# Local attention scores over zero-padded keys, and linear attention's float32 products in two column halves

## The chip, the cores and the metric

The kernel runs on one core of one Trainium2 chip. The metric is device microseconds (us) of the whole program, the median of several executions. Engines are named as in the profile: PE is TensorE's matmuls, PEld its weight loads (the stationary operand), DVE VectorE, ACT ScalarE, POOL GpSimd, SP SyncE. "Records" are the instructions that the profiler saw: a float32 matmul of the program leaves two matmul records and two weight loads, a float32r matmul leaves one of each.

## The reference, cut to what matters

512 tokens of width 1024 go through a token-mixing block, a product-key expert layer, a gated delta rule layer and a short convolution layer. The change is in the first of these. There, the normed input is projected to many parts, and two kinds of attention are formed from them:

```python
# gated linear attention, 4 heads, dk 128, dv 256, chunks of 64 tokens
def step(state, xs):
    qi, ki, vi, di = xs
    out = jnp.einsum('bhtd,bhde->bhte', qi, state)
    state = di[..., None] * state + jnp.einsum('bhsd,bhse->bhde', ki, vi)
    return state, out
o = o_intra + o_inter            # o_intra = (masked q k) v inside a chunk
...
# sliding window attention, 16 heads of 64 sharing 4 key heads, blocks of 128 tokens
s = jnp.einsum('bnqhgd,bnkhd->bnhgqk', qb, kk) * (hd ** -0.5)   # kk: this block's keys and the last one's
...
p = jnp.exp(s - m)
```

Their outputs are gated, projected, merged and added to the stream.

## The kernel before

The function `mix` holds both attentions. Most large products are made from two float32r parts of each operand (a first part and the remainder), three matmuls a product, in `mm3` (L207, L208, L209); the weights come from DRAM into `wraw` and are split into `whi` on ACT (L89) and `wlo` on DVE (L92).

**Linear attention.** For each of the 4 heads, `gla_inside` forms what needs no state: cumulative gates (L353), masked scores (L378), keys transposed (L383). Then `gla_chunks` walks through 4 token tiles of two chunks each. Per tile it makes, all in plain float32: the product inside the chunks (L394, stationary 128 x 128, 256 columns moving, 16 in all), for each chunk the product of queries with the state (L398, stationary 128 x 64: its 64 result rows lie on half of the array's columns, 28 in all), and for each chunk the state's update (L402, its 64 tokens lie on half of the array's rows, 64 x 128 stationary, 28 in all). DVE adds the decayed state (L408), ACT evacuates (L412, L413). The order in this stage isn't written out by hand: a scheduler interleaves the projections that come later in the program (`tokspill`, through `mm3`) with the heads.

**Sliding window attention.** The keys' two float32r parts are kept feature-major in a tile `kp_`: `kh_`, the first part, is there twice, on both halves of the partitions; `kl_`, the second part, is there once, on partitions 0 to 63 for key heads 0 and 1 and on 64 to 127 for key heads 2 and 3. A query's two parts lie on the two halves of `qT`. So a score is made by one matmul over 128 partitions (L552: both parts of the query with the keys' first part) and a second over 64 (L553: the query's first part with the keys' second part):

```python
PE.matmul(b, qT[:, i], kh_[:, hg, ks], start=True, stop=False)
PE.matmul(b, qT[half_(w), i], kl_[half_(w), hg % 2, ks], start=False, stop=True)
```

`weights` does this for four heads, eight matmuls one after the other; it is called 16 times, of which 4 (block 0) have 128 key columns and 12 have 256. The keys are written by `read_keys` (transposes L504, ACT L507 for `kh_`, DVE L510 for `kl_`). In this stage the order on PE is written out by hand (`manual_schedule`, L639): 18 slots, in each `spread` (transposes of the weights of two slots earlier, L584), `queries_out` (L538, then ACT L541), `attend` (L599, L601), `weights`, and between these a fixed number of `mm3` steps of the gates' projections (`fill`). After the scores of a slot come DVE copies (L561, L562), the maximum, the exponentials on ACT (L574), and the scaling on POOL (L578), which the transposes of the second slot after wait for. The last projections in the stage (`out_steps`) use ACT's Silu (L622).

POOL fills the masked scores' tiles (L374), block 0's score tiles (L559) and takes the queries' second part (L532).

Of the kernel before, what the change touches and what calls it, by code (L numbers as in the profile page):

```python
# [16 lines left out]
P = 128  # L17
T = 512
# [11 lines left out]
def kernel(ctx: ExitStack, tc: tile.TileContext, A: dict, out: bass.AP):  # L30
# [24 lines left out]
    # ---------------------------------------------------------------- helpers  # L55
# [21 lines left out]
    share = {"every": 0, "n": 0}    # of the weights' second parts, every n-th by the pool engine  # L77

    def wchunk(ap, name="w"):
        """A [128, 2048] chunk of a weight matrix (8 row tiles, 256 columns) in two halves, each split  # L80
        into two float32r parts. For a token-major product the halves are along the rows, for a
        feature-major one along the columns."""
        for i in range(NK // HK):
            raw = wraw.tile([P, HK * 256], F32, name=name + "raw", tag="wraw")
            hi = wsp.tile([P, HK * 256], F32R, name=name + "hi", tag="whi")
            lo = wsp.tile([P, HK * 256], F32R, name=name + "lo", tag="wlo")
            with tc.high_priority(offset=WPRIO):
                nc.sync.dma_start(raw, ap[:, i * HK * 256:(i + 1) * HK * 256])
                S.activation(hi, raw, AF.Copy)  # L89
                share["n"] += 1  # L90
                pool_ = share["every"] and share["n"] % share["every"] == 0
                (GP if pool_ else V).tensor_tensor(lo, raw, f32(hi), op=ALU.subtract)  # L92
            yield i, hi, lo
# [4 lines left out]
    def rsqrt(ss, n, shape, name="rs", dst=None):  # L98
        """1/sqrt(ss*n + eps): a first guess from the exponent's bits, then Newton steps."""
# [16 lines left out]
    def rsqrt2(ss, n, name, dst=None):  # L116
        """the same for two columns on the pool engine, by its power"""
# [11 lines left out]
    def evac_split(hi, lo, p, scale):  # L129
        """hi + lo = p * scale, in two float32r parts."""  # L130
# [5 lines left out]
    class Stream:  # L136
        """The residual stream between two stages, [128, 4, 1024] token-major: in SBUF, in DRAM, 1/rms
        of every token, and the normed stream transposed, in two parts [128, 8, 512]. n: the stage
        that reads it."""
# [12 lines left out]
        def squares(self, tiles):  # L152
            """the sums of squares of every token of two token tiles"""
# [6 lines left out]
        def ready(self, t, ss):  # L160
            """token tiles t and t + 1 are complete; ss: their sums of squares"""
# [6 lines left out]
        def norm(self, t):  # L168
            """token tile t, normed and transposed"""
# [20 lines left out]
        def first_feat(self, ap, order=(0, 1)):  # L190
            """The token tiles of the second half, and proj_feat of the first chunk by halves."""
            w = [(m, *kview(x, NK)) for m, *x in wchunk(ap)]
            pp = [pj() for m in range(2)]
            for j in order:
# [4 lines left out]
                # The first start clears the whole bank.  # L199
# [28 lines left out]
    def proj_tok_last(aps, xs):  # L228
        """proj_tok whose token tiles end one after the other; yields them by pairs."""
# [22 lines left out]
    def proj_feat_steps(ap, xh, xl, by, n=T):  # L252
        """feature-major: [128 features, n tokens] for the two column tiles of a chunk."""
# [9 lines left out]
    def proj_tok_steps(aps, xs, by):  # L263
        """token-major: four [128 tokens, 256 columns]; aps: the chunks along K, xs: their operands."""
# [4 lines left out]
        # Two groups share a bank: the first matmul's start clears the whole bank, and the second  # L269
        # group's first write finds it cleared.  # L270
# [12 lines left out]
    # ---------------------------------------------------------------- token mixing  # L283
    def mix(X, O):
        w1 = A["w_in"]
        with ExitStack() as st:
# [56 lines left out]
            # ---- gated linear attention, head by head  # L343
# [5 lines left out]
            def gla_inside(h):  # L349
                """the parts of a head that need no state"""  # L350
# [35 lines left out]

            def gla_chunks(h, qx, ket, at, dec):
# [4 lines left out]
                for t in range(NT):  # L392
                    po = ps()[:, :256]
                    PE.matmul(po, at[:, t, :], gv[:, t, h * 256:(h + 1) * 256], start=True, stop=True)  # L394
                    for a in range(2):
                        n = 2 * t + a
                        if st_ is not None:
                            PE.matmul(po[64 * a:64 * a + 64, :], qx[:, n, :], st_, start=False,  # L398
                                      stop=True, skip_group_check=True)
                        if n < 7:  # L400
                            sp = ps()[:, :256]
                            PE.matmul(sp, ket[64 * a:64 * a + 64, t * P:(t + 1) * P], vh(t, a),  # L402
                                      start=True, stop=True)
# [41 lines left out]
            # ---- sliding window attention  # L445
# [31 lines left out]
            # Keys and queries in two float32r parts, feature-major: the keys' first part twice, on either  # L477
            # half of the partitions, and a query's two parts on the two halves; so one pass gives two of
            # the three products, and a second one the third. The second key head pair has the halves
            # swapped, for its keys' second part lies on the other half.  # L480
            kp_ = s16([P, 6, T], F32R, name="kp")
            kh_, kl_ = kp_[:, 0:4], kp_[:, 4:6]
# [12 lines left out]
            def read_keys(t):  # L495
# [12 lines left out]
                for w in range(2):  # L508
                    o, h = half_(w), slice(2 * w, 2 * w + 2)
                    V.tensor_tensor(kl_[o, :, s], p[o, h], f32(kh_[o, h, s]), op=ALU.subtract)  # L510
# [33 lines left out]
            def weights(n, hg, qT):  # L544
                """the softmax of four heads that share keys; the columns hold the tokens of block n up to the
                row and those of block n - 1 after it"""
                w = hg // 2
                sp = [ps(), ps()]
                ks = slice(max(0, n - 1) * P, (n + 1) * P)
                for i in range(4):  # L550
                    b = sp[i // 2][:, (i % 2) * 256 + (0 if n else P):(i % 2) * 256 + 256]
                    PE.matmul(b, qT[:, i], kh_[:, hg, ks], start=True, stop=False)  # L552
                    PE.matmul(b, qT[half_(w), i], kl_[half_(w), hg % 2, ks], start=False, stop=True)  # L553
# [50 lines left out]
            # ---- branch gates, output gate of the linear attention  # L604
# [31 lines left out]
            # Four heads a slot: their scores in one slot, the weighted sums two slots later; the tensor  # L636
            # engine's work in a fixed order, with the gates' projections in between.
# [31 lines left out]
            # ---- branches, merge  # L669
# [39 lines left out]
    # ---------------------------------------------------------------- product-key experts  # L709
    def peer(X, O):  # L710
        KD = 3                      # token tiles that go through all experts on the tensor engine
        ND = KD * P
        HS = 16                     # tokens of a staged block of gate matrices
        TB = 4                      # tokens of a block of one-hot rows
        with ExitStack() as st:
# [19 lines left out]
            # ---- the last token tile: its experts' rows by indirect DMA  # L735
# [37 lines left out]
            # ---- the other tiles through all experts: groups of five chunks, ten rows of experts  # L773
# [57 lines left out]
            # ---- scores and the 16 best keys of every head and half  # L831
# [36 lines left out]
            def route(t):  # L868
                """the 16 best experts of every head, their gates; yields every few operations"""
# [3 lines left out]
                # pairs (a, b) with (a+1)(b+1) <= 16: every other pair has 16 better or earlier ones  # L873
# [35 lines left out]
                # gates  # L909
# [21 lines left out]
                # indices and the gate's two parts, one row per (head, k), as float16  # L931
# [7 lines left out]
            def gate_matrices(t):  # L939
                """G[j, i] of every token of the tile, expert i * 128 + j"""  # L940
# [26 lines left out]
            # the tensor engine's projections at an even rate in between  # L967
# [41 lines left out]
    # ---------------------------------------------------------------- gated delta rule  # L1009
    def out_proj(aps, parts, X, O, wr, Y=None):  # L1010
        """X + rmsnorm(the projection (+ Y)) * w; aps[c]: the weights of 256 columns."""
# [38 lines left out]
    def conv_silu(p, wc, taps, tmp):  # L1050
        """Causal depthwise convolution along the free axis, one weight per partition and tap."""
# [7 lines left out]
    def gdn(X, O):  # L1059
# [6 lines left out]
        with ExitStack() as st:  # L1066
# [23 lines left out]
            # ---- keys and queries, feature-major and not normed: [dk, head, chunk, (k | q), 64]  # L1090
# [6 lines left out]
            def kq_mm(i):  # L1097
                """one tile of 128 columns of the projection; i: pair of key heads, (k, q), key head"""
# [26 lines left out]
            # ---- beta and g, token-major [128, 4, 16]  # L1125
# [53 lines left out]
            def g_rows():  # L1179
                # E[j, (h, t), i] = exp(G_i - G_j) for j <= i, else 0  # L1180
# [37 lines left out]
            def u_store(c, q):  # L1218
                """the diagonal blocks of U of key heads 2c and 2c + 1"""
# [8 lines left out]
            def rows(c):  # L1228
                """the factors of every token of key heads 2c and 2c + 1"""
# [56 lines left out]
            # ---- values (filler of the triangular solve)  # L1286
# [94 lines left out]
            # ---- R = (I + U)^-1: 32 x 32 diagonal blocks by substitution, (half, head, tile) on  # L1381
            # partitions
# [18 lines left out]
            # to rows on partitions by the tensor engine; the first block's transpose too  # L1401
# [12 lines left out]
            # the off-diagonal blocks: -R1 U12 R2; the two halves' blocks on a diagonal  # L1414
# [42 lines left out]
            # ---- the recurrence, two heads of a key head at a time  # L1457
# [27 lines left out]
            def recur(kh, vb, kd, oo):  # L1485
                """The chunks of a pair of heads; yields after each step that waits for another engine."""
# [90 lines left out]
            # Two pairs at a time, half a pair apart; the tensor engine's work in a fixed order, with  # L1577
            # the steps of the output gate's and the output's projections in between.
# [18 lines left out]
            def fill(x):  # L1597
                """the projections' steps up to the time x of the plan"""
# [44 lines left out]
    # ---------------------------------------------------------------- short convolution  # L1643
# [168 lines left out]
```

## Time and profile before

| | |
|---|---|
| median of 3 runs | 3065.36 us (3063.47, 3065.36, 3077.59) |
| profiled execution, first to last instruction | 3072.8 us |
| mean granted TensorE clock | 0.983 of full speed |
| PE busy / PEld / DVE / ACT / POOL | 96% / 81% / 64% / 40% / 22% |
| PE matmul records | 16274 |
| linear attention's chunks | about 141 to 203 us of the span |
| sliding window stage | about 255 to 460 us |

The profile holds one execution; no other time of it is recorded than its span. The share of busy time is over the whole span, and a busy PE is not PE at its peak: matmuls overlap, and the end of one is modelled. What a matmul costs in a row of matmuls is the distance from its start to the start of the next, which the timeline shows.

### The profile page before, as it was taken

Reading aid. Unit: us, or ns where it says so; the run is one execution under the profiler, and the core shown is the slowest. Engines: PE = TensorE matmul, PEld = TensorE weight load, DVE = VectorE, ACT = ScalarE, POOL = GpSimd, SP = SyncE. Lnnn points to the kernel's source line nnn. Section 1 sums busy time; section 2 is a strip of 40 time slices with the busy share of each in tenths; the row PEclk is TensorE's granted clock in tenths of the full one; section 3 lists DMA queues with packets and bytes.
Section 4 is the critical chain, followed back from the end, with each engine's and each line's share of the span. In section 5 each row is a group of like instructions: output and inputs, shape, how many; then the busy total and the mean of one; then the engine's idle time right before and its main releaser. Section 6 shows DMA issues by size and latency. Waiting matters only on the chain.

```text
span 3072.8 us, 42867 instructions
## 1 busy us (share of the span) xinstructions
PE 2943.9 (96%) x16274; PEld 2499.6 (81%) x16274; DVE 1972.4 (64%) x3798; ACT 1216.1 (40%) x2089; POOL 662.6 (22%) x583
## 2 busy tenths in 40 slices
PE   8999999998889999999899999999999999999998
PEld 6978778888889998777798888787866678888888
DVE  3348664499898776777787777658845554444432
ACT  3534473323345553333333333465343344332322
POOL 1001110002342312223454443134411202000000
PEclk9999999999999999999999999999999899999999
DMA  3213224333466779899999888446322313223222
GB/s 130 76 58 131 85 86 157 106 100 100 143 217 226 244 267 307 315 333 317 323 315 313 308 320 309 160 115 144 128 86 90 107 59 119 98 96 124 96 90 83
DMA packets 206919, 528.61 MB, mean 172 GB/s; under 512 B 38777, under 2 KB 84441, under 8 KB 202362
## 3 DMA queue, kind: packets, MB, share of 16 engines
q1 hardware_dynamic: 144018, 326.17, 32.5%
q0 software_dynamic: 43168, 155.27, 14.2%
q10 hardware_dynamic: 19528, 44.44, 3.9%
q8 instruction: 128, 2.10, 0.3%
q14 instruction: 77, 0.63, 0.1%
HBM read 464.49 MB, written 61.33 MB: 171 GB/s over the span
## 4 chain that ended last, share of the span: by engine, by line
PE 50%; DMA 9%; DVE 6%; issue 4%; ACT 2%; POOL 1%; SPq 0%; POOLq 0%; DVEq 0%; ACTq 0%
PE pp L207 12%; PE pp L208 11%; PE pp L209 11%; DMA wraw<-in_peer_v_dram 4%; DMA gath<-in_peer_v_rows_dram,ge 2%; PE ps L209 2%; PE ps L208 2%; PE ps L207 2%; DVE wlo L92 1%; PE ps L1495 1%; PE ps L1529 1%; DMA gath<-in_peer_u_rows_dram,ge 1%; DMA wraw<-in_peer_u_dram 1%; PE ps L954 1%; POOL gath L751 1%
## 5 line engine op out<-in xcount | busy, mean ns | idle before, releaser
L89 ACT ACTIVATE whi<-wraw 128x1024 fp32r<-128x1024 f32 x492 | 519.9, 1057 | 980.1 <-PE pp L208 555.1
L92 DVE TENSOR_TENSOR wlo<-wraw,whi 128x1024 fp32r<-128x1024 f32 x466 | 580.3, 1245 | 422.6 <-ACT whi L89 409.7
L209 PE MATMUL pp<-x2h,wlo 128*128 128x384 f32 (+2 forms) x1168 | 405.4, 347 | 23.7 <-DVE wlo L92 22.0
L207 PE MATMUL pp<-x2h,whi 128*128 128x384 f32 (+2 forms) x1168 | 407.6, 349 | 17.3 <-ACT whi L89 9.7
L208 PE MATMUL pp<-x2l,whi 128*128 128x384 f32 (+2 forms) x1168 | 404.2, 346 | 1.1 <-DVE x2l L188 1.1
L209 PE MATMUL ps<-whi,wtl 128*128 128x512 f32 x640 | 254.8, 398 | 8.5 <-DVE wtl L817 8.5
L208 PE MATMUL ps<-wlo,wth 128*128 128x512 f32 x640 | 254.9, 398 | 3.2 <-DVE wlo L92 3.2
L207 PE MATMUL ps<-whi,wth 128*128 128x512 f32 x640 | 253.8, 397 | 2.3 <-ACT whi L89 2.0
L209 PEld LDWEIGHTS pp<-x2h,wlo 128*128 128x128 f32 x1168 | 224.8, 193 | 34.7 <-DVE wlo L92 28.1
L751 POOL DMA_INDIRECT gath<-in_peer_u_rows_dram,ge x128 | 173.3, 1354 | 336.2 <-DVE gath L754 168.6
L207 PEld LDWEIGHTS pp<-x2h,whi 128*128 128x128 f32 x1168 | 225.3, 193 | 24.2 <-ACT whi L89 10.8
L751 POOL DMA_INDIRECT gath<-in_peer_v_rows_dram,ge x128 | 170.1, 1329 | 316.9 <-DVE gath L754 153.7
L208 PEld LDWEIGHTS pp<-x2l,whi 128*128 128x128 f32 x1168 | 225.2, 193 | 6.5 <-DVE x2l L188 1.6
L207 PE MATMUL pp<-x4h,whi 128*128 128x512 f32 (+1 forms) x528 | 202.4, 384 | 3.8 <-ACT x4h L187 3.8
L208 PE MATMUL pp<-x4l,whi 128*128 128x512 f32 (+1 forms) x528 | 202.7, 384 | 0.9 <-DVE x4l L188 0.9
L209 PE MATMUL pp<-x4h,wlo 128*128 128x512 f32 (+1 forms) x528 | 202.5, 384 | 0.0
L759 DVE SCALAR_TENSOR_TENSOR acc<-gath,w,acc 128x1024 f32<-128x1024 f32 x127 | 163.7, 1289 | 22.7 <-DMA gath<-in_peer_v_rows_dram,ge 22.5
L754 DVE SCALAR_TENSOR_TENSOR gath<-gath,grow 128x1024 f32<-128x1024 f32 x128 | 157.4, 1237 | 30.0 <-DMA gath<-in_peer_u_rows_dram,ge 29.8
L207 PE MATMUL pp<-x3h,whi 128*128 128x512 f32 (+1 forms) x400 | 168.4, 421 | 7.4 <-ACT x3h L187 5.7
L816 ACT ACTIVATE wth<-wt 128x384 fp32r<-128x384 f32 x128 | 66.8, 522 | 252.1 <-PE pp L208 154.5
L208 PE MATMUL pp<-x3l,whi 128*128 128x512 f32 (+1 forms) x400 | 156.4, 391 | 1.8 <-DVE x3l L188 1.8
L209 PE MATMUL pp<-x3h,wlo 128*128 128x512 f32 (+1 forms) x400 | 156.3, 391 | 0.0
(492 smaller groups left out, 6500.2 us busy)
## 6 DMA issues: line engine op xcount, KB each, us to landing
wraw<-in_peer_u_dram SPq DMA_DIRECT2D x128, 512.0 KB, 5.3
wraw<-in_peer_v_dram SPq DMA_DIRECT2D x128, 512.0 KB, 7.1
wraw<-in_sc_w_in_dram SPq DMA_DIRECT2D x64, 512.0 KB, 3.5
wraw<-in_w_in_dram SPq DMA_DIRECT2D x52, 512.0 KB, 4.0
Gd<-sgs ACTq DMA_DIRECT2D x24, 1024.0 KB, 6.5
wraw<-in_gdn_w_in_dram SPq DMA_DIRECT2D x48, 512.0 KB, 3.7
Gt<-Gd SPq DMA_DIRECT2D x12, 1920.0 KB, 15.8
Hd<-ht ACTq DMA_DIRECT2D x25, 384.0 KB, 4.5
```

What stands on the lines that cost most here:

```text
L89: S.activation(hi, raw, AF.Copy)
L92: (GP if pool_ else V).tensor_tensor(lo, raw, f32(hi), op=ALU.subtract)
L207: PE.matmul(p, lh, rh, start=first, stop=False, skip_group_check=skip)
L208: PE.matmul(p, lh, rl, start=False, stop=False, skip_group_check=skip)
L209: PE.matmul(p, ll, rh, start=False, stop=last, skip_group_check=skip)
L751: GP.indirect_dma_start(out=r, out_offset=None, in_=src, in_offset=bass.IndirectOffsetOnAxis(ap=idx3[:, k:k + 1], axis=0))
L754: V.scalar_tensor_tensor(r, r, 1.0, xn3, op0=ALU.mult, op1=ALU.mult, accum_out=h3[:, k:k + 1])
L759: V.scalar_tensor_tensor(acc3, r, w3[:, k:k + 1], acc3, op0=ALU.mult, op1=ALU.add)
L816: S.activation(wh, w, AF.Copy)
L954: PE.matmul(o, AB[:, 1, :, q], A2[:, 0, :, q], start=True, stop=False)
L1495: PE.matmul(B2[o, 0, v], Q[s_][o, u, :], vn[o, v], start=True, stop=True)
L1529: PE.matmul(B2[:, 1, v], kd[o, v, t, :], vn[o, v], start=True, stop=True)
```

## The change

Three things change, all in `mix`. The second part of the keys gets a slot for each of the four key heads, is filled with zeros by POOL, and is then written on the same half of the partitions as before; so the second product of a score runs over all 128 partitions, with the zero half adding nothing. The three float32 products of `gla_chunks` are each issued as two matmuls of 128 columns. Comments and docstrings are removed, which is not shown.

```diff
+            cols = [slice(0, P), slice(P, 2 * P)]
...
                     po = ps()[:, :256]
-                    PE.matmul(po, at[:, t, :], gv[:, t, h * 256:(h + 1) * 256], start=True, stop=True)
+                    for j, c in enumerate(cols):
+                        PE.matmul(po[:, c], at[:, t, :], gv[:, t, h * 256:(h + 1) * 256][:, c], start=j == 0,
+                                  stop=True, skip_group_check=True)
                     for a in range(2):
                         n = 2 * t + a
                         if st_ is not None:
-                            PE.matmul(po[64 * a:64 * a + 64, :], qx[:, n, :], st_, start=False,
-                                      stop=True, skip_group_check=True)
+                            for c in cols:
+                                PE.matmul(po[64 * a:64 * a + 64, c], qx[:, n, :], st_[:, c], start=False,
+                                          stop=True, skip_group_check=True)
                         if n < 7:
                             sp = ps()[:, :256]
-                            PE.matmul(sp, ket[64 * a:64 * a + 64, t * P:(t + 1) * P], vh(t, a),
-                                      start=True, stop=True)
+                            for c in cols:
+                                PE.matmul(sp[:, c], ket[64 * a:64 * a + 64, t * P:(t + 1) * P], vh(t, a)[:, c],
+                                          start=True, stop=True)
...
-            kp_ = s16([P, 6, T], F32R, name="kp")
-            kh_, kl_ = kp_[:, 0:4], kp_[:, 4:6]
+            kp_ = s16([P, 8, T], F32R, name="kp")
+            kh_, kl_ = kp_[:, 0:4], kp_[:, 4:8]
+            GP.memset(f32(kl_), 0.0)
...
                 for w in range(2):
                     o, h = half_(w), slice(2 * w, 2 * w + 2)
-                    V.tensor_tensor(kl_[o, :, s], p[o, h], f32(kh_[o, h, s]), op=ALU.subtract)
+                    V.tensor_tensor(kl_[o, h, s], p[o, h], f32(kh_[o, h, s]), op=ALU.subtract)
...
             def weights(n, hg, qT):
-                w = hg // 2
...
                     PE.matmul(b, qT[:, i], kh_[:, hg, ks], start=True, stop=False)
-                    PE.matmul(b, qT[half_(w), i], kl_[half_(w), hg % 2, ks], start=False, stop=True)
+                    PE.matmul(b, qT[:, i], kl_[:, hg, ks], start=False, stop=True)
```

## Rows read from the trace of the kernel before

**Rows 1.** Busy time in three stretches: us, busy time (records) of each engine, PEclk, DMA.

```profile
145.00:205.00 60.00, 59.57 (x312) 36.51 (x311) 32.58 (x86) 24.61 (x71) 2.74 (x8) 1.00 0.10 33
255.00:460.00 205.00, 204.24 (x1068) 155.65 (x1067) 137.79 (x351) 112.03 (x278) 29.07 (x33) 1.00 0.29 94
460.00:520.00 60.00, 60.00 (x266) 49.35 (x265) 30.20 (x38) 23.00 (x31) 0.00 (x0) 1.00 0.50 172
```

**Rows 2.** Timeline of PE, a slot's scores: start us, us, line, out<-in, shapes.

```profile
386.88 0.39 PE L209 MATMUL pp<-x1h,wlo 128*128 128x512 f32 x1
387.11 0.28 PE L552 MATMUL ps<-kp,qT 128*128 128x256 f32 x1
387.32 0.38 PE L553 MATMUL ps<-kp,qT 64*128 64x256 f32 x1
...
389.50 0.50 PE L207 MATMUL pp<-x1h,whi 128*128 128x512 f32 x1
389.84 0.40 PE L208 MATMUL pp<-x1l,whi 128*128 128x512 f32 x1
```

**Rows 3.** Timeline of PE, float32r matmuls of 256 columns one after the other.

```profile
153.31 0.28 PE L207 MATMUL pp<-whi,x1h 128*128 128x256 f32 x1
153.43 0.28 PE L208 MATMUL pp<-wlo,x1h 128*128 128x256 f32 x1
```

**Rows 4.** Line L553: records, ns min/median/max, first and last start, forms.

```profile
L553 PE MATMUL ps<-kp,qT x64: 323/380/381, 266.2 to 436.3; 64*128 64x256 f32 x48, 64*128 64x128 f32 x16
```

**Rows 5.** Timeline of PE, scores of a slot of block 0 and what follows.

```profile
266.08 0.22 PE L552 MATMUL ps<-kp,qT 128*128 128x128 f32 x1
...
268.36 0.40 PE L208 MATMUL pp<-x1l,whi 128*128 128x512 f32 x1
```

**Rows 6.** Timeline of PE, four float32r matmuls of 128 columns and what follows.

```profile
262.18 0.56 PE L538 MATMUL ps<-identr,qs 128*128 128x128 f32 x4
...
262.86 0.40 PE L208 MATMUL pp<-x1l,whi 128*128 128x512 f32 x1
```

**Rows 7.** Lines L394, L398, L402, columns as in Rows 4.

```profile
L394 PE MATMUL ps<-gv,gat x32: 379/380/484, 141.7 to 200.5; 128*128 128x256 f32 x32
...
L398 PE MATMUL ps<-gst,ge x56: 379/404/431, 143.5 to 203.2; 128*64 128x256 f32 x56
...
L402 PE MATMUL ps<-gv,gket x56: 376/428/480, 142.2 to 201.7; 64*128 64x256 f32 x56
```

**Rows 8.** Timeline of PE and PEld, chunks of a head.

```profile
161.97 0.70 PE L402 MATMUL ps<-gv,gket 64*128 64x256 f32 x4
...
162.60 0.70 PE L394 MATMUL ps<-gv,gat 128*128 128x256 f32 x2
...
163.23 0.65 PE L398 MATMUL ps<-gst,ge 128*64 128x256 f32 x2
...
163.81 0.29 PEld L402 LDWEIGHTS ps<-gv,gket 64*128 64x128 f32 x2 [0.39 <-issue]
```

**Rows 9.** Timeline of PE, float32 matmuls of 128 columns one after the other.

```profile
158.25 1.16 PE L378 MATMUL ps<-gqi,gki 128*128 128x128 f32 x8 [0.22 <-DVE gki L366]
159.16 0.36 PE L209 MATMUL pp<-whi,x1l 128*128 128x256 f32 x1
```

**Rows 10.** Timeline of PE and POOL, a late slot's softmax and its transposes.

```profile
437.41 1.04 POOL L578 TENSOR_TENSOR se<-se,ssm 128x512 f32<-128x512 f32 x1 [10.43 <-DVE ssm L577]
...
438.51 0.66 PE L584 MATMUL ps<-ident,se 128*128 128x128 f32 x4 [0.22 <-POOL se L578]
```

**Rows 11.** Timeline of POOL; then the first writes of the keys' tile.

```profile
251.62 0.74 POOL L532 TENSOR_TENSOR qs<-sq,qs 128x256 fp32r<-128x256 f32 x1 [47.38 <-ACT qs L531]
...
L507 ACT ACTIVATE kp<-ps x4: 575/594/599, 258.9 to 333.3; 128x512 fp32r<-128x512 f32 x4
```

**Rows 12.** Timeline of PE, projections under a head's inside.

```profile
172.76 0.36 PE L208 MATMUL pp<-wlo,x1h 128*128 128x256 f32 x1
...
178.00 1.16 PE L378 MATMUL ps<-gqi,gki 128*128 128x128 f32 x8 [0.21 <-DVE gki L366]
```

## The prediction

> **What bounds the kernel now.** I read the page first: PE is busy 96% of the span, so I take PE as the bound where nothing speaks against it, and look at the two stages that the change touches by themselves. The table by stretches [rows 1] shows PE busy 59.57 of 60 us in the linear attention, 204.24 of 205 in the sliding window stage and all of the 60 us after it, at a granted clock of 1.00, with DVE at two thirds or less and the DMA engines at 50% or less. So in both stages, and behind them, time goes as PE goes, and us that PE saves should move everything after it forward. But a busy PE can be busy with little: what a matmul costs is the distance between starts, so the third view is the timeline of PE.
>
> There the reader is to see one thing. In the scores [rows 2], L552 (128 rows of the array) and L553 (64 rows) alternate. From the first L553 at 387.32 to the L207 at 389.50 are seven starts in 2.18 us, 0.311 each. Projections of the same 256 columns and the same type, all over 128 rows, start every 0.12 [rows 3]. So every change between 64 and 128 rows costs about 0.19. It is a constant and no matter of columns: in block 0 seven steps with 128 columns take 0.26 each by the same reading (266.08 to 268.36 with the first step and the last taken off) [rows 5], 0.05 less for 128 columns less, which is the stream alone.
>
> **The change, part by part.**
>
> Scores over 128 rows. The whole block of a slot, from the first L552 at 387.11 to the L208 at 389.84, is 2.73 us. An L209 takes 0.23 (386.88 to 387.11), and one projection's step of that size lies in the block, so the scores cost 2.50. After the change all eight are like those of [rows 3]: 8 x 0.12 = 0.96. A slot saves 1.54. L553 has 48 records of 256 columns and 16 of 128 [rows 4], four a slot: 12 slots save 12 x 1.54 = 18.5 us. In block 0 the scores cost 266.08 to 268.36, less 0.23: 2.05. Four float32r matmuls of 128 columns over 128 rows, with their exit, take 262.18 to 262.86 less 0.23: 0.45 [rows 6]; eight take 0.90 at most. Four slots save 4 x 1.15 = 4.6. Together **23.1 us**. The zero half is streamed with the rest and costs nothing of its own: a pass takes as long as its columns, with 64 rows or 128.
>
> Halved float32 products. A whole L402 from start to start is 162.60 minus 161.97 = 0.63, and an L394 the same (162.60 to 163.23); an L398 is 0.58 (163.23 to 163.81) [rows 8]. Each has neighbours of another shape, so the constant is in it: with 0.20 for it, two records of 256 columns stream 0.43. Records of 128 columns in a row start every (159.16 - 158.25) / 8 = 0.114 [rows 9], four of them 0.456. So a halved product costs about 0.03 more, if its second, third and fourth weight loads go under the matmuls before them, as the second does now: both loads of an L402 are over 0.29 after the start [rows 8], long before the first matmul's 0.2 us of stream, which begins behind the first load, has ended. There are 16, 28 and 28 products (records of [rows 7] halved): 72 x 0.03 = **2.2 us** lost. From below it is nothing: the columns are the same. From above, every extra load lies open. The 64-column load of L398 makes its step 0.05 shorter than that of L402, so a load of 128 columns is open for 0.10 and one of 64 for 0.05, and what is left of the constant, 0.10, is the emptying of the array. Two more loads for each product: 44 x 2 x 0.10 + 28 x 2 x 0.05 = 11.6 more.
>
> The Trainium skill weighs here. "TensorE: Matmul & The Clock Gate", Part 3, section "The mechanism", says that a weight load overlaps running matmuls only where it goes to another row group. By that rule the extra loads, which go to their own matmul's rows, would all lie open, and the sum would lose the 11.6 us. [Rows 8 and 9] speak against it here, since loads of the same rows run ahead, and I leave it to a rival.
>
> The pair. At 161.97 four records of L402 start in one 0.63 step [rows 8]: two chunks on the two halves of the rows run at once. The trace has five such pairs. With halves issued one chunk after the other they may overlap less: nothing from below, 5 x 0.34 = 1.7 from above (the second chunk's last three of four records, 0.114 each, no longer covered). I take half, **0.8**.
>
> The fill with zeros. POOL gets one more instruction of 2048 columns. No row shows this fill; POOL's heavier L578 takes 1.04 for 512 columns [rows 10], so 4.2 us is a bound from above, nothing from below. POOL is idle for 47.38 us before 251.62 [rows 11], and the tile is first written at 258.9 in the kernel before, so it is hidden: I take zero. If that cover were gone, DVE's L510 and with it the first scores would be late by up to 4.2 us, once. The tile has the size of a slot of its pool's others, and DVE's L510 writes as many elements as before.
>
> What is queued behind. Slots become 1.5 us shorter while ACT, DVE and POOL do the same work in them. Most of their chain starts when the scores end, so it moves with them; only what spans the next slot's scores has less time. That is the scaled softmax, L578, which the transposes need two slots on. In one late slot, where ACT also has the Silu work, it is late already: L584 waits 0.22 for an L578 that ends at 438.45 [rows 10]. There the 1.54 saved in the slot between turn into a wait: **1.5 us** given back. From below nothing, from above the same in the last four slots, 4 x 1.54 = 6.2.
>
> The sum: 23.1 - 2.2 - 0.8 - 1.5 = 18.6 us saved. The profiled execution's span is 3072.8; nothing else of it is recorded, and it is 7.4 (0.24%) above the median of the runs, 3065.36, as one execution among runs that lie 14 us apart. The saving is in us and the same in both: 3054 for the span, 3065.4 - 18.6 = **3046.8** for the median, 0.61% less.
>
> **Rivals.**
>
> *Open loads.* The extra weight loads of the halved products aren't covered, where the array works in halves. For it: with a change of shape just before, the first load is open now. Against it: the second loads are not [rows 8]. Time: 18.6 - 11.6 = 7.0 saved, 3058.4. With the pairs' upper bound too, 3059.3.
>
> *The softmax chain takes over* in the last four slots: 23.1 - 2.2 - 0.8 - 6.2 = 13.9 saved, 3051.5. For it is the wait that is there [rows 10]; against it, that PE waits 0.8 us in the whole of that stage (205 less 204.24) [rows 1], so the other slots have slack.
>
> *Slower: the scheduler's order.* The linear attention isn't ordered by hand, and it has 72 more matmuls to place. Now the waits inside a head (DVE and ACT between L353 and L378) are covered by projections, 172.76 to 178.00 [rows 12], 5.2 us a head. If the new order put these projections elsewhere, PE would stand idle there: with all four heads open 21.0 us, 18.6 - 21.0, or 3067.8. It decides from 18.6 / 5.2 = 3.6 heads on, that is only with all four. Against it: PE has 0.4 us idle in 60 there now [rows 1], and the halves become ready together with their partners.
>
> **How the numbers follow.** A measurement of this kernel can tell some 0.5% from no change, 15 us: faster means under 3050, slower over 3081. The forecast gets 0.74, with its own range 3041 to 3051 (all its losses at nothing give 3042.3). Open loads 0.12, the softmax chain 0.08, the order 0.06. The forecast and its near neighbours and a little of the chain's case lie under 3050: faster 0.71. Slower 0.05, for the order with a clock that falls in the idle stretches, which I can't price from these rows. The rest, 0.24, is the same. The range has the forecast, the chain and the open loads: from 3040 (two us under the 3042.3, as two of the three runs lie 1.9 apart) to 3060.
>
> **What would show it.** Right: L552 and L553 start every 0.12 (0.10 or so in block 0), with L553 over 128 rows; the stage from the first L538 to the merge is some 21 us shorter; L394 and L402 keep steps near 0.65, L398 near 0.60. Open loads would show as steps near 0.85 for L394 and L402. The chain would show as PE's waits for L578 in the late slots. A wrong order would show as idle PE between 130 and 205 us. The forecast fails if the float32r matmuls on one result bank, by turns with two moving operands and one stationary, can't start every 0.12, for which I have only the projections as witness.

## The result, and the profile after

The changed kernel takes 3052.72 us (median of 20 runs, 3040.35 to 3068.88); the kernel before, beside it on the same chip, 3068.84 (median of 19 runs, the three first ones among them; a twentieth took 6191.61 and is left out as slow). The ratio is 0.9948, with a 95% interval of 0.9933 to 0.9964: some 16 us, or 0.52%, faster. The prediction was 3046.8 in a range of 3040 to 3060. Its saving of 18.6 us lies inside the interval (11 to 21 us). Of the 5.9 us between the two times 3.5 are the kernel before itself, whose median of 19 lies that far above the 3065.36 of its first three runs, and 2.5 are a smaller saving.

Where the time came from is read from three marks: the first product inside a chunk, the first transpose of the keys, and the first transpose of the next layer's stream. They are the first starts of three lines, here of the kernel after:

```profile
L398 PE MATMUL ps<-gv,gat x64: 275/275/377, 144.1 to 211.5; 128*128 128x128 f32 x64
L513 PE MATMUL ps<-ident,kd x16: 270/272/296, 267.1 to 335.3; 128*128 128x128 f32 x16
L182 PE MATMUL ps<-ident,x2s x32: 272/272/273, 578.1 to 593.3; 128*128 128x128 f32 x32
```

and of the kernel before (the first mark is the L394 of [rows 7], 141.7):

```profile
L504 PE MATMUL ps<-ident,kd x16: 271/272/328, 258.3 to 333.0; 128*128 128x128 f32 x16
L182 PE MATMUL ps<-ident,x2s x32: 272/272/273, 589.3 to 604.5; 128*128 128x128 f32 x32
```

The linear attention's stretch grew from 116.6 to 123.0 us (+6.4), the stretch of the scores and all behind them shrank from 331.0 to 311.0 (-20.0): together -13.6. The two profiled executions differ by 18.5 (3072.8 and 3054.3). Of the other 4.9 us, 7.3 lie in later layers that the change doesn't touch, and 2.4 of the other sign lie ahead of the first mark, where the granted clock differs between the two executions (0.91 in after, 0.96 in before, between 60 and 100 us). Single executions of one kernel differ by more than that: the 20 runs of after span 28.5 us. So I read the parts from these two stretches and leave the whole to the runs.

The clock that each run lists bears the 13.6 us out. A straight line of time against mean granted clock, with one slope for both kernels, fitted to the 52 runs of before that stand beside the experiments and the 20 of after, puts after 13.6 us under before, with a 95% interval of 12 to 16. So the saving is nearer to 14 us than to the 16 of the ratio, and the forecast's 18.6 was too much.

The scores, to be held against [rows 2], and those of block 0, against [rows 5], from PE's timeline of the kernel after:

```profile
353.87 0.28 PE L560 MATMUL ps<-kp,qT 128*128 128x256 f32 x1
353.99 0.28 PE L561 MATMUL ps<-kp,qT 128*128 128x256 f32 x1
354.11 0.28 PE L560 MATMUL ps<-kp,qT 128*128 128x256 f32 x1
...
355.05 0.40 PE L208 MATMUL pp<-x1l,whi 128*128 128x512 f32 x1
```

```profile
274.86 0.22 PE L560 MATMUL ps<-kp,qT 128*128 128x128 f32 x1
...
275.99 0.40 PE L208 MATMUL pp<-x1l,whi 128*128 128x512 f32 x1
```

The starts are 0.12 apart. A block is 1.18 long, less the 0.23 of the projection in it: 0.95, and in block 0 1.13 - 0.23 = 0.90.

The chunks of the linear attention, as in [rows 8]:

```profile
144.06 0.61 PE L398 MATMUL ps<-gv,gat 128*128 128x128 f32 x4
144.60 0.72 PE L409 MATMUL ps<-gv,gket 64*128 64x128 f32 x8
145.25 0.49 PE L398 MATMUL ps<-gv,gat 128*128 128x128 f32 x2
145.82 0.65 PE L404 MATMUL ps<-gst,ge 128*64 128x128 f32 x4
146.40 0.49 PE L398 MATMUL ps<-gv,gat 128*128 128x128 f32 x2
146.82 0.48 PE L409 MATMUL ps<-gv,gket 64*128 64x128 f32 x2
```

Two things are to be seen. Eight records of L409, two whole products on the two halves of the rows, still take one step, 144.60 to 145.25. And L398, the product inside the chunks, appears with two records where a whole product has four: one half stands by itself between products of other shapes.

Busy time in stretches (columns as in [rows 1]) and PE's waits, first between 255 and 460 us, then between 110 and 260 (who waited, for whom, us in total, times, longest), of the kernel after:

```profile
145.00:205.00 60.00, 57.64 (x405) 47.71 (x403) 29.59 (x69) 21.59 (x61) 3.93 (x7) 0.97 0.13 41
255.00:440.00 185.00, 181.50 (x1072) 148.61 (x1072) 138.51 (x367) 106.48 (x276) 30.36 (x34) 1.00 0.31 100
```

```profile
PE ps L592 <- POOL se L586: 2.4, 2, 1.9
PE ps L607 <- DVE spc L595: 0.6, 1, 0.6
PE ps L560 <- ACT qT L550: 0.5, 1, 0.5
```

```profile
PE ps L378 <- DVE gki L366: 2.8, 3, 1.9
```

and the last of these in the kernel before:

```profile
PE ps L378 <- DVE gki L366: 1.1, 3, 0.7
```

L592 is the old L584, which waited 0.2 us for the softmax before [rows 10]; now it waits 2.4. And PE has 2.36 us idle in the 60 us of the linear attention, where it had 0.43 [rows 1]. That place was not in the forecast. What happened there, from the timeline of POOL, DVE and PE:

```profile
177.79 1.81 POOL L491 MEMSET kp<- 128x2048 f32 x1
177.82 1.80 DVE L103 TENSOR_SCALAR grm<-gss 128x4 f32<-128x4 f32 x1 [1.53 <-ACT gjk L419]
...
184.77 1.17 PE L378 MATMUL ps<-gqi,gki 128*128 128x128 f32 x8 [1.87 <-DVE gki L366]
185.95 0.42 PE L207 MATMUL pp<-whi,x1h 128*128 128x256 f32 x1
186.17 0.41 PE L208 MATMUL pp<-wlo,x1h 128*128 128x256 f32 x1
...
189.15 0.28 PE L207 MATMUL pp<-whi,x1h 128*128 128x256 f32 x1
189.27 0.28 PE L208 MATMUL pp<-wlo,x1h 128*128 128x256 f32 x1
```

The fill with zeros runs in a hole of POOL's work inside a head. A DVE instruction of 4 columns that starts 0.03 us behind it takes as long as the fill, and a few us later PE stands idle for DVE. Behind the idle time the projections start every 0.21 us, from 189.15 on every 0.12. Between the two the granted clock is 0.50, the lower of its two levels (1.2 GHz):

```profile
185.95:189.15 3.20, 3.20 (x16) 3.20 (x16) 2.23 (x4) 0.63 (x1) 0.00 (x0) 0.50 0.58 181
```

### The profile page after: what moved, and what is told of

Read it like the earlier page. It is cut to its first block, busy times and chain, and to the rows that moved or that the text cites. A ratio compares the mean times of both kernels' runs of the same rounds, so it can differ in the third digit from the quotient of the medians.

```text
span 3054.3 us, 43160 instructions
## 1 busy us (share of the span) xinstructions
PE 2925.1 (96%) x16418; PEld 2509.7 (82%) x16418; DVE 1973.9 (65%) x3798; ACT 1214.6 (40%) x2089; POOL 665.0 (22%) x584
## 4 chain that ended last, share of the span: by engine, by line
PE 52%; DMA 8%; DVE 6%; issue 3%; ACT 2%; POOL 1%; DVEq 0%; POOLq 0%; ACTq 0%
PE pp L207 13%; PE pp L208 12%; PE pp L209 12%; DMA wraw<-in_peer_v_dram 4%; PE ps L209 3%; PE ps L207 3%; PE ps L208 3%; DMA wraw<-in_peer_u_dram 2%; DMA gath<-in_peer_v_rows_dram,ge 2%; DVE wlo L92 1%; PE ps L1503 1%; PE ps L962 1%; PE ps L1537 1%; PE ps L963 1%; PE ps L1518 1%
## 5 line engine op out<-in xcount | busy, mean ns | idle before, releaser
L92 DVE TENSOR_TENSOR wlo<-wraw,whi 128x1024 fp32r<-128x1024 f32 x466 | 583.1, 1252 | 420.1 <-ACT whi L89 419.3
```

## The experiments

Three questions stand behind the runs. Do the scores gain by the change of shape that goes, or by the rows that are filled up? Are the 6.4 us in the linear attention the halves' alone, and then their weight loads or their order? Or is it the fill that holds DVE, with the rival that both only happen to fall together? The lengths of the two stretches in this table come from one profile of each kernel, read as above.

| kernel | median us (runs) | ratio, 95% interval | linear attention | scores and behind |
|---|---|---|---|---|
| before | 3068.84 (19), 3067.55 (29), 3066.03 (23) | | 116.6 | 331.0 |
| after | 3052.72 (20) | 0.9948 [0.9933, 0.9964] | 123.0 | 311.0 |
| keys_only | 3053.80 (12) | 0.9965 [0.9940, 0.9990] | 119.8 | 311.0 |
| halves_only | 3070.70 (12) | 1.0022 [1.0004, 1.0041] | 119.9 | 331.0 |
| grouped64 | 3051.24 (12) | 0.9953 [0.9934, 0.9972] | 116.7 | 315.4 |
| padded | 3037.25 (6) | 0.9924 [0.9898, 0.9950] | 109.9 | 311.0 |
| keys_early | 3050.99 (12) | 0.9946 [0.9923, 0.9970] | 116.6 | 311.1 |
| fill_twice | 3038.06 (1) | | 122.4 | 311.0 |
| shape_order | 3035.82 (6) | 0.9900 [0.9863, 0.9938] | 106.0 | 311.1 |
| shape_order_halves | 3049.13 (12) | 0.9930 [0.9902, 0.9958] | 106.3 | 311.1 |

The first median of before belongs to after, the second to keys_only, halves_only, grouped64 and padded, the third to the others from keys_early on. In the two kernels with a fixed order the updates of the state come ahead of the first product inside a chunk; from the first product of either kind their stretches are 106.6 and 107.0.

**keys_only**: the change without the halves.

```diff
-                    for j, c in enumerate(cols):
-                        PE.matmul(po[:, c], at[:, t, :], gv[:, t, h * 256:(h + 1) * 256][:, c], start=j == 0,
-                                  stop=True, skip_group_check=True)
+                    PE.matmul(po, at[:, t, :], gv[:, t, h * 256:(h + 1) * 256], start=True, stop=True)
```

and the two other products in the same way.

> The keys padded to 128 partitions, linear attention as before. Theory (every change between 64 and 128 rows costs about 0.2 us, and PE is the bound): L552 and L553 start every 0.12 us with 256 columns; from the first key transpose (L504) to the first transpose of the next layer's stream (x2s) the span is some 20 us shorter, and the whole about 20 us, 0.65% faster. The linear attention, from its first L394 to the first key transpose, stays at the 116.6 us of before. Rival (the gain of the change came from both edits, or partly from chance): clearly less than 16 us here.

The scores' stretch is that of after, 311.0. The linear attention is not back at 116.6: 119.8, so 3.2 us are lost without any halved product. The fill is again beside L103, which takes 1.80 us (174.43) instead of 0.17. By the stretches the kernel saves 16.8 us; its ratio says 11, with an interval of 3 to 18, so the 20 us of the expectation were too many by either reading.

**halves_only**: the kernel before with the three products halved as in the change, keys untouched.

> Only the halved float32 products, the scores as before. Theory: no product costs more by being halved, but the scheduler puts other products between two halves: 16 more groups of one shape on PE (88 for 72), 0.2 us each, 3 us, and a longer idle stretch inside a head with the clock falling behind it, up to 3 us; so from the first intra-chunk product to the first key transpose 3 to 7 us longer, and the whole 0.1 to 0.2% slower. Rival (open weight loads): steps of 0.85 us for four records of L394 and L402, 12 us or more. Rival (nothing): unchanged within 1 us.

The linear attention takes 119.9, 3.3 more than before, and the median is 3.15 above before's; the ratio's interval, 1 to 13 us slower, holds both. PE's idle time doesn't account for it, as it is 0.74 us in this window, 0.31 more than in [rows 1]:

```profile
145.00:205.00 60.00, 59.26 (x424) 48.68 (x424) 30.49 (x78) 22.73 (x66) 2.18 (x6) 1.00 0.11 35
```

The two losses add up: 3.3 + 3.2 = 6.5, against 6.4 in after.

**grouped64**: the kernel before, with the scores' eight matmuls in two groups of one shape. The second still runs over 64 rows, so the zero padding is not needed; only the number of changes between 128 and 64 rows falls, from seven to one inside a block.

```diff
                 for i in range(4):
-                    PE.matmul(b, qT[:, i], kh_[:, hg, ks], start=True, stop=False)
-                    PE.matmul(b, qT[half_(w), i], kl_[half_(w), hg % 2, ks], start=False, stop=True)
+                    PE.matmul(bs[i], qT[:, i], kh_[:, hg, ks], start=i % 2 == 0, stop=False, skip_group_check=True)
+                for i in range(4):
+                    PE.matmul(bs[i], qT[half_(w), i], kl_[half_(w), hg % 2, ks], start=False, stop=True,
+                              skip_group_check=True)
```

> The kernel before, its second products still over 64 partitions, but a slot's four first products are issued before its four second ones. Theory (the cost is the change of shape): two changes a slot in place of eight, so the scores of a slot with 256 columns go from 2.50 us to about 1.4, and 16 slots save some 18 us, of which 2 to 3 are given back in late slots: 15 to 18 us faster in all. Rival (a product over 64 partitions is slow in itself, by 0.38 us a pair): nothing saved.

PE's timeline of a block:

```profile
357.35 0.63 PE L552 MATMUL ps<-kp,qT 128*128 128x256 f32 x4
357.91 0.74 PE L554 MATMUL ps<-kp,qT 64*128 64x256 f32 x4
358.58 0.50 PE L207 MATMUL pp<-x1h,whi 128*128 128x512 f32 x1
358.92 0.39 PE L208 MATMUL pp<-x1l,whi 128*128 128x512 f32 x1
```

A block takes 1.57 - 0.23 = 1.34 us: between the 2.50 of before and the 0.95 of after, and what is left over the 0.95 is two changes of shape, 0.39 or 0.195 each. The stretch is 315.4, so 15.6 of the 20.0 us come without any padding. What the padding removes is the change of shape, not the work of 64 rows.

**padded**: keys_only, and the linear attention's products made 128 x 128 too. The operands with 64 columns or 64 rows get zeros beside them, in one tile filled once ahead of the heads.

```diff
-                            PE.matmul(po[64 * a:64 * a + 64, :], qx[:, n, :], st_, start=False,
+                            PE.matmul(po, qx[:, t, a:a + 2, :].rearrange("p a c -> p (a c)"), st_, start=False,
...
-                            PE.matmul(sp, ket[64 * a:64 * a + 64, t * P:(t + 1) * P], vh(t, a),
+                            PE.matmul(sp, ket[:, t, a, :], gv[:, t, h * 256:(h + 1) * 256],
```

> Keys padded, and the linear attention's products padded too: the state's update over 128 tokens with zero rows for the other chunk, the product with the state with zero columns for the other chunk, all 128 by 128, not halved. Theory: the constant goes from these too; 72 products at 0.43 us, 31 us, for some 41 now: the stretch from the first L394's place to the first key transpose 8 to 10 us shorter than in the kernel before, and the whole 28 to 30 us, 0.9 to 1%, faster than before. Rival (the state's chain through DVE is the bound in there, and a constant gone turns into waiting): the stretch not shorter by more than 3 us, the whole like keys padded alone.

```profile
145.69 0.59 PE L408 MATMUL ps<-gv,gat 128*128 128x256 f32 x2
146.12 0.59 PE L412 MATMUL ps<-gst,gpad 128*128 128x256 f32 x2
```

A product takes 0.43 us, where steps with a change of shape took 0.58 to 0.63 [rows 8]; the stretch is 109.9, 6.7 under before's, although no two updates can run at once any more. That is less than the 8 to 10 that were expected; where the rest went stays open. The keys' fill is in this kernel as well (177.84 to 179.65), but it holds nothing there: DVE has no instruction ready beside it and waits 1.52 us for PE.

**keys_early**: keys_only, with the keys' tile and its fill moved ahead of the linear attention.

```diff
             gv = s16([P, NT, D], name="gv")
+            kp_ = s16([P, 8, T], F32R, name="kp")
+            kh_, kl_ = kp_[:, 0:4], kp_[:, 4:8]
+            GP.memset(f32(kl_), 0.0)
```

(and taken out where it was.)

> Keys padded, linear attention as before, but the keys' tile is taken and filled with zeros ahead of the linear attention, where DVE has little to do. Theory (the 1.81 us fill on POOL holds up one DVE instruction in the chain inside a head, and PE's idle stretch there brings the clock down): DVE's L103 takes 0.17 us everywhere, PE waits about 0.7 us for L366 at most, the clock stays up around 190 us, and the stretch from the first L394 to the first key transpose is 116.6 us as before the change, for 119.8 with the late fill; from the first L353 to the next layer's first transpose 445.6 us. Rival (the 3.2 us come from the scheduler's order, which the new instruction changed): 119 to 120 again.

The timeline of POOL and DVE, and PE's waits between 110 and 260 us:

```profile
18.36 1.81 POOL L339 MEMSET kp<- 128x2048 f32 x1
17.93 1.59 DVE L92 TENSOR_TENSOR wlo<-wraw,whi 128x1024 fp32r<-128x1024 f32 x1
19.44 0.68 DVE L188 TENSOR_TENSOR x1l<-ps,x1h 128x512 fp32r<-128x512 f32 x1
...
172.72 0.17 DVE L103 TENSOR_SCALAR grm<-gss 128x4 f32<-128x4 f32 x1 [1.66 <-ACT gjk L418]
```

```profile
PE ps L381 <- DVE gki L369: 1.1, 3, 0.7
```

The same fill at another place costs nothing: L103 is back at 0.17, PE's waits for DVE at the 1.1 us of before, the granted clock from 145 to 205 at 1.00, and the linear attention at 116.6. It isn't that DVE has nothing to do there: L92 and L188 run beside the fill, and take no longer than in the kernel before (1.58 and 0.68). So it matters which instruction of DVE stands beside a fill; the TENSOR_TENSORs here weren't held, the TENSOR_SCALAR L103 was.

**fill_twice**: keys_only with the fill issued twice, one behind the other; the result of the second is that of the first.

> Keys padded as in the change, linear attention as before, and the zeros written twice, one fill right behind the other; the rest is the same. Theory (the fill holds up DVE): a second DVE instruction, or the same one, is held for another 1.8 us, PE's wait for L366 grows from 1.8 to some 3.5 us, and the stretch to the first key transpose from 119.8 to 121 to 123 us. Rival (order, not the fill): 119.8 again, with L103 as it was.

The timeline of POOL and DVE, and PE's waits between 110 and 260 us:

```profile
173.07 1.81 POOL L487 MEMSET kp<- 128x2048 f32 x1
173.11 1.80 DVE L103 TENSOR_SCALAR grm<-gss 128x4 f32<-128x4 f32 x1 [1.66 <-ACT gjk L415]
174.94 1.81 POOL L488 MEMSET kp<- 128x2048 f32 x1
174.94 1.83 DVE L104 TENSOR_SCALAR grt<-grm 128x4 int32<-128x4 int32 x1
```

```profile
PE ps L378 <- DVE gki L366: 4.3, 3, 3.5
```

Each fill holds one DVE instruction of 4 columns for as long as it runs, and PE's longest wait for L366 goes from keys_only's 1.8 us to 3.5. The stretch is 122.4, 5.8 above keys_early's against 3.2 with one fill. The single time of 3038.06 says nothing on this: it is one execution, and its later layers were short (2460.7 us behind the third mark, against 2483.5 in before).

**shape_order**: keys_early, with the products of a token tile in a fixed order: both updates of the state, the product inside the chunks, then both products with the state. All products are whole.

```diff
-                            if st_ is not None:
-                                PE.matmul(po[64 * a:64 * a + 64, :], qx[:, n, :], st_, start=False,
...
+                    with tc.manual_schedule(engines={nc.tensor.engine}):
+                        for n in ns:
...
+                                PE.matmul(sps[n][:, c], ket[64 * a:64 * a + 64, t * P:(t + 1) * P], vh(t, a)[:, c],
+                                          start=True, stop=True)
...
+                            PE.matmul(po[:, c], at[:, t, :], gv[:, t, h * 256:(h + 1) * 256][:, c], start=j == 0,
...
+                            sts[n + 1] = st_ = sn
+                        for n in (2 * t, 2 * t + 1):
...
+                                    PE.matmul(po[64 * a:64 * a + 64, c], qx[:, n, :], sts[n][:, c], start=False,
```

> Keys padded and filled early; linear attention's products whole, but each token tile's in a fixed order by shape: both state updates, the product inside the chunks, both products with the state. Theory (a constant of 0.2 us for each group of a shape, and products on different halves of the array run at once): 53 groups for 72 in the part of PE's queue around the heads, 3.8 us, and more pairs at once, 3 us for the updates and up to 5 for the products with the state: 105 to 110 us from the first product to the first key transpose, for 116.6. Rival (the wait for DVE between a pair's products takes it all back): 115 us or more.

```profile
147.05 0.70 PE L408 MATMUL ps<-gv,gket 64*128 64x256 f32 x4
147.69 0.70 PE L411 MATMUL ps<-gv,gat 128*128 128x256 f32 x2
148.31 0.66 PE L425 MATMUL ps<-gst,ge 128*64 128x256 f32 x4
148.90 0.70 PE L408 MATMUL ps<-gv,gket 64*128 64x256 f32 x2
```

Both updates take one step of 0.64 (147.05 to 147.69) and so do both products with the state, 0.59. Around the heads PE's order has 53 groups of one shape in this kernel, against 72 in before. The stretch is 106.0 us, and the kernel has the lowest ratio of all here, 1.0% under before; its interval just touches that of after.

**shape_order_halves**: the same order with each product as two of 128 columns.

```diff
-                cs_ = [slice(0, 256)]
+                cs_ = cols
```

> The same fixed order as in shape_order, with each float32 product issued as two of 128 columns right behind each other. It shows what halving costs when no other product comes in between. Theory: nothing to 0.03 us a product, so within 2 us of shape_order in the stretch to the first key transpose. Rival (weight loads open, or pairs that no longer run at once): 5 us or more longer than shape_order.

```profile
146.11 0.72 PE L408 MATMUL ps<-gv,gket 64*128 64x128 f32 x8
146.76 0.71 PE L411 MATMUL ps<-gv,gat 128*128 128x128 f32 x4
147.40 0.66 PE L425 MATMUL ps<-gst,ge 128*64 128x128 f32 x8
148.00 0.71 PE L408 MATMUL ps<-gv,gket 64*128 64x128 f32 x4
```

The steps are 0.65, 0.64 and 0.60 against 0.64, 0.62 and 0.59, the stretch 106.3 against 106.0: with the order held, halving 72 products costs 0.3 us. The medians of the two lie further apart (13 us), but the intervals of their ratios overlap, and the stretches of this layer show no such difference.

## Why the prediction was right, and where it was wrong

**The scores** (23.1 us) were right, by their mechanism and their size. The steps are the 0.12 forecast, the blocks 0.95 and 0.90 against 0.96 and 0.90. grouped64 shows the mechanism by itself: the cost belongs to the change of shape. That it is "a constant and no matter of columns" was misread, though: in block 0, with 128 columns, a step with changes takes 0.26 and one without 0.11 (0.90 / 8), so a change costs 0.15 there and not 0.19. Without changes, matmuls of 128 columns start only 0.01 closer to each other than those of 256. The sum did not suffer, because block 0 was costed from its own rows.

**The softmax chain** (1.5 us given back) was the right place, mis-sized. PE waits 3.5 us between 255 and 460, 2.7 more than before's 0.76 [rows 1], most of it for POOL's L586, in two waits and not in one. 23.1 - 2.7 = 20.4, and the marks show 20.0. The rival in which it takes over (6.2) did not come.

**The halved products** (2.2 us) and **the pair** (0.8) were wrong in their mechanisms, though their sum of 3.0 is near the 3.3 of halves_only. The cost of the halves themselves is nearly nil: 0.3 us for 72 products, by shape_order and shape_order_halves. Pairs still run at once, eight records of L409 in 0.65 us; after has four such groups and four of six records, where before had five pairs. What costs is the order. The scheduler put other products between the halves of one: the groups of one shape around the heads rose from 72 to 88, in after and in halves_only alike, and 16 more changes at 0.19 make 3.0 us, against 3.3 measured. The 0.19 can be read in this stage itself: a half of L398 that stands alone takes 0.42 (146.40 to 146.82 above), and two records of 128 columns in a row take 0.23 [rows 9]. That it is the order is shown, as the cost goes away where the order is fixed; that it is these 16 changes is worked out. The rival on the scheduler's order thus held in its cause, not in its mechanism: the projections stayed under the heads' insides, and the waits there did not grow in halves_only.

**Open loads** fell: steps of halved products are 0.65 and 0.58 in after, and 0.64 for L411 in shape_order_halves, not the 0.85 that this rival asked for. The rule from the Trainium skill ("TensorE: Matmul & The Clock Gate", Part 3, "The mechanism") that stood behind that rival does not agree with the runs here, where 72 products cost 0.3 us by being halved; the measurement decides.

**The fill with zeros** is the step that failed. It was costed at nothing, hidden under POOL's idle time before the keys [rows 11], and bounded by 4.2 us at the keys' first writes. It cost 3.2 us, at another place. The 47 us of [rows 11] are the idle time of POOL, and POOL wasn't the engine to look at: the fill, which waits for nothing there, was placed in the middle of a head, and DVE, which is on the head's chain, stood for its whole 1.81 us. The chain was late by as much: PE's waits for L366 went from 1.1 to 2.8 us, 1.7 more. Behind the longest, 1.87 us, the granted clock fell to the lower level, and 15 projections from 185.95 to 189.15 took 3.20 us instead of 15 x 0.12 = 1.80, 1.4 more. Together that is 3.1 in after, beside the 3.2 of keys_only. keys_early and fill_twice show the cause from both sides. A changed order is not behind it: keys_only has 72 groups of one shape around the heads, as before. That the clock fell because of the idle time is what the order of the rows says; no run changes the one without the other.

The Trainium skill has a rule for this, "SBUF — State Buffer", "Who interferes with whom": DVE and GpSimd share one pair of ports, which is an exclusive lock, and a tensor_scalar in a mode with two ports is blocked for as long as GpSimd's whole instruction where that was issued first. The traces agree: 1.80 and 1.83 us of L103 and L104 beside fills of 1.81, and 0.17 without one. Which mode these two ran in, no row shows.

The sum by the runs is 23.1 - 2.7 - 3.3 - 3.2 = 13.9 us, and 13.6 by the marks; 18.6 was forecast. The forecast was 4.7 us too high by this sum: 3.2 from the fill, 1.2 from the softmax chain and 0.3 from the halved products and the pair. That the time still lies in the range owes to the range's width of 20 us as much as to the steps. A time under 3050, which had 0.71, did not come.

## What to carry to other kernels

Count changes of array shape in PE's queue before counting columns: in the scores each cost 0.19 us with 256 columns and 0.15 with the 128 of block 0, and putting matmuls of one shape side by side brought most of what padding brings, without the padding. An instruction on an idle engine is free only if it holds nothing that a busy engine needs: ask where a fill that waits for nothing will be placed and which instruction of DVE will stand beside it, and issue it where no chain passes. And where a scheduler sets the order, splitting an instruction gives it a place to put something in between, so the cost of a split is read from the new order, not from the split.

## What the runs showed of the hardware

A fill of 2048 float32 columns on POOL took 1.81 us and held a DVE TENSOR_SCALAR of 128 x 4 for 1.80 us in float32 and 1.83 in int32 (fill_twice); beside the early fill of keys_early a TENSOR_TENSOR of 128 x 512 took 0.68, as without one.

The time of one kernel moves with the granted clock, by more than the change is worth: two executions of before took 3085.43 us at a mean clock of 0.978 and 3048.59 at 0.987, and a straight line through its 52 runs beside the experiments gives 2.5 us for each 0.001 of mean clock. A part of it sits in the third layer, far behind the change. Here are 60 us from the same place of that layer, in before and in the profiled execution of shape_order (columns as in [rows 1]):

```profile
2384.80:2444.80 60.00, 56.88 (x261) 37.91 (x262) 28.58 (x81) 21.81 (x63) 12.51 (x21) 0.83 0.37 114
```

```profile
2352.60:2412.60 60.00, 57.32 (x204) 37.69 (x204) 23.40 (x64) 16.95 (x51) 11.24 (x20) 0.61 0.37 112
```

The granted clock is 0.83 and 0.61, and PE gets 261 and 204 records done. From that layer's first transpose to the end, the profiled execution of shape_order took 1124.0 us and that of before 1108.0. The whole of it took 3058.61, 22.8 above the median of its own runs, though its first stages were among the shortest. Why the clock falls further in one execution than in another, no run here shows.
